# Two transformer blocks on one core: other places for three kinds of work, and two heads' last products in turn

## The chip, the core and the metric

The kernel runs on one core of a Trainium2 chip. The metric is device time in microseconds (us), the median of several executions. Five engines work side by side, each through its own list of instructions in a fixed order: TensorE (PE, matmuls; its weight loads are shown apart as PEld), VectorE (DVE), ScalarE (ACT), GpSimd (POOL) and SyncE (SP, which only issues transfers). [...]

## The reference

Two blocks of two layers each follow each other on 512 tokens of 1024 features. A layer of the first block mixes tokens in three branches (a gated matrix memory, a linear recurrence, sparse attention), merges them and applies a feed-forward network; a layer of the second block attends (over itself and over 256 memory tokens) and applies another one.

```python
for l in range(2):                                   # first block
    h = rms_norm(x, norm_mix[l]);  p = h @ w_in[l]   # split into 14 parts
    y_a = mlstm(...);  y_b = gelu(r_g) * rg_lru(conv(r_x), ...)   # recurrence: a scan over tokens
    score = sum_h w[t,h] * relu(q_idx[t,h] . k_idx[s])            # top 128 keys of each token
    y_c[h] = softmax(mask(q[h] @ k[h].T / 8)) @ v[h]              # 8 heads of 64 features
    x = x + (g_a*(y_a@wb0) + g_b*(y_b@wb1) + g_c*(y_c@wb2)) @ w_out[l]
    h = rms_norm(x, norm_ffn[l]);  g, u = split(h @ ffn_up[l])    # 2 x 3072
    x = x + (gelu(conv(g)) * u) @ ffn_down[l]
x = rms_norm(x, norm_final);  mem_n = rms_norm(mem, mem_norm)     # 256 x 1024
for i in range(2):                                   # second block
    x = x + concat(mixer(x), memory_attention(x, mem_n @ w_mem_kv[i])) @ w_out[i]
    g, u = split(rms_norm(x, norm_ffn[i]) @ w_gate_up[i])         # 2 x 2816
    x = x + (silu(g) * u) @ w_down[i]
```

## The kernel before

Features lie on the 128 partitions and tokens along the free axis, so x is eight tiles of 128x512. Each large product is made in three passes: operand and weight are split into a high part (`wh`, made on ACT, line 361) and a rest (`wl`, DVE, line 369), and `three` (line 436) issues rest by high, high by rest and high by high (line 433). Small exact products go through `mm32` (line 421), transposes through `turn` (line 425). Weights come in pieces of 128x1024 into 8 buffers `raw`; a piece is split into one of 3 pairs `wh`, `wl` some units ahead of its use.

The order on every engine is made while the program is built. Each piece of work is a generator (a chain) with a priority (a low number goes first). `Issue` holds the operations that are ready, with a cost from a formula for each helper (`scan` has 0.00104 us an element, `mm32` four passes at 2400 columns a us), and always issues the one that can start first by these costs, among near equals the one of the best priority. So a cost or a priority changes the order everywhere behind it. `main` (in `drive`) issues the units of weights one after the other, in the order in which `body` yields them; `loader` and `splitter` run up to 8 units ahead.

The feed-forward network (`ffn`, line 1969) multiplies a block of 256 columns of gate and up with 7 products instead of 8 (units P1 to P7, 24 matmuls each). P1, P5, P6 and P4 of a block use one buffer: after the split for P1, `dma_add` (line 416, on the queue of POOL) adds another piece of weights to it in place, P5 can be split when that has landed, and so on. When two blocks are done, their four tiles `ff` are the operand of the second projection (`down_units`, ps_t): its pieces of 24 matmuls (two output tiles, four operand tiles) are put between later P units, at the places that the list `first` gives.

`dsa_pair` (line 1554) handles two of the eight sparse heads: scores ps_at (the two heads in turn, on partitions 0 to 63 and 64 to 127 of the operands), probabilities `pr`, transposes ps_pt into `pT`, products ps_y with `av`; head 0 writes partitions 0 to 63 of the bank ps_y, head 1 the others. `rg_chain` (line 1317) is the recurrence; its products are ps_rg. `mem_prep` (line 2113) prepares the memory: four loads, a norm, 16 transposes ps_mem. ps_st and ps_bc are the sums of squares and the spreading of a norm.

## Time and profile before

| | |
|---|---|
| median of 3 runs | 3227.7 us (3225.82 to 3227.99) |
| the profiled execution | 3223.32 us, its span 3221.5 us |
| PE busy | 3167.3 us, 98% of the span |
| DVE, ACT, POOL busy | 2305.4, 1587.9, 403.3 us (72%, 49%, 13%) |
| share of the chain that ended last | PE 86%, DVE 9%, issue 2%, ACT 1% |
| moved by DMA | 397.39 MB, mean 123 GB/s |

PE is the engine to look at: 54.2 us of the span are left in which it does not work. Times in the rows further down are us from the start of the span unless ns is said. A line of the timeline gives start, duration, engine, line, output and inputs, shape and count, and in brackets how long the engine was idle before and what ended that.

### The profile page before, as it was taken

Reading aid. Unit: us, or ns where it says so; the run is one execution under the profiler, and the core shown is the slowest. Engines: PE = TensorE matmul, PEld = TensorE weight load, DVE = VectorE, ACT = ScalarE, POOL = GpSimd, SP = SyncE. Lnnn points to the kernel's source line nnn. Section 1 sums busy time; section 2 is a strip of 40 time slices with the busy share of each in tenths; the row PEclk is TensorE's granted clock in tenths of the full one; section 3 lists DMA queues with packets and bytes.
Section 4 is the critical chain, followed back from the end, with each engine's and each line's share of the span. In section 5 each row is a group of like instructions: output and inputs, shape, how many; then the busy total and the mean of one; then the engine's idle time right before and its main releaser. Section 6 shows DMA issues by size and latency. Waiting matters only on the chain.

```text
span 3221.5 us, 47254 instructions
## 1 busy us (share of the span) xinstructions
PE 3167.3 (98%) x18213; PEld 2712.2 (84%) x18213; DVE 2305.4 (72%) x4454; ACT 1587.9 (49%) x2650; POOL 403.3 (13%) x439
## 2 busy tenths in 40 slices
PE   8999999999999999999999999999999999999999
PEld 6778778989987778778989988888999988889998
DVE  7974444777787974445778787787777767777775
ACT  6552433544445552334544456877443457664443
POOL 2000000211100010000211112120211211011110
PEclk9999999999999999999999999999999999999999
DMA  5323233777752323233878753232887742257883
GB/s 155 98 73 92 68 90 101 156 169 159 175 142 76 105 72 92 67 98 98 167 162 175 167 133 118 62 99 57 173 176 165 185 151 72 66 115 173 176 175 82
DMA packets 367249, 397.39 MB, mean 123 GB/s; under 512 B 18031, under 2 KB 341344, under 8 KB 367024
## 3 DMA queue, kind: packets, MB, share of 16 engines
q1 hardware_dynamic: 262256, 276.47, 28.1%
q0 software_dynamic: 104736, 117.90, 21.9%
q8 instruction: 143, 2.34, 0.3%
q14 instruction: 82, 0.67, 0.1%
q10 hardware_dynamic: 32, 0.01, 0.0%
HBM read 383.83 MB, written 10.49 MB: 122 GB/s over the span
## 4 chain that ended last, share of the span: by engine, by line
PE 86%; DVE 9%; issue 2%; ACT 1%; DMA 0%; SPq 0%; POOL 0%; DVEq 0%; POOLq 0%; ACTq 0%
PE ps_t L433 38%; PE ps_u L433 26%; PE ps_n L433 11%; PE ps_at L433 2%; DVE wl L369 2%; PE ps_y L433 2%; PE ps_pt L425 2%; PE ps_y L421 1%; DVE m L1243 1%; DVE score L1244 1%; DVE u L369 1%; ACT pr L361 1%; DVE pr L1551 1%; PE ps_num L421 1%; PE ps_S L421 1%
## 5 line engine op out<-in xcount | busy, mean ns | idle before, releaser
L361 ACT ACTIVATE wh<-raw 128x1024 fp32r<-128x1024 f32 (+2 forms) x671 | 698.0, 1041 | 1020.0 <-PE ps_t L433 496.5
L369 DVE TENSOR_TENSOR wl<-raw,wh 128x1024 fp32r<-128x1024 f32 (+2 forms) x671 | 804.9, 1200 | 474.1 <-ACT wh L361 470.1
L433 PE MATMUL ps_u<-xsh,wl 128*128 128x256 f32 x1472 | 415.9, 283 | 11.0 <-DVE wl L369 8.0
L433 PE MATMUL ps_u<-xsh,wh 128*128 128x256 f32 x1472 | 414.9, 282 | 0.0
L433 PE MATMUL ps_u<-xsl,wh 128*128 128x256 f32 x1472 | 414.8, 282 | 0.0
L433 PE MATMUL ps_t<-ffl,wh 128*128 128x512 f32 x736 | 293.2, 399 | 3.8 <-DVE ffl L369 3.7
L433 PE MATMUL ps_t<-ffh,wl 128*128 128x512 f32 x736 | 289.1, 397 | 6.3 <-ACT ffh L361 5.7
L433 PE MATMUL ps_t<-ffh,wh 128*128 128x512 f32 x736 | 291.6, 396 | 0.0
L433 PEld LDWEIGHTS ps_u<-xsh,wl 128*128 128x128 f32 x1472 | 278.6, 189 | 13.7 <-issue 7.8
L433 PE MATMUL ps_t<-h2h,wl 128*128 128x512 f32 x704 | 280.6, 399 | 0.0
L433 PE MATMUL ps_t<-h2h,wh 128*128 128x512 f32 x704 | 280.3, 398 | 0.0
L433 PE MATMUL ps_t<-h2l,wh 128*128 128x512 f32 x704 | 279.9, 398 | 0.0
L433 PEld LDWEIGHTS ps_u<-xsl,wh 128*128 128x128 f32 x1472 | 278.6, 189 | 0.0
L433 PEld LDWEIGHTS ps_u<-xsh,wh 128*128 128x128 f32 x1472 | 278.6, 189 | 0.0
L369 DVE TENSOR_TENSOR x<-x,ps_t 128x512 f32<-128x512 f32 x232 | 158.2, 685 | 154.5 <-PE ps_t L433 152.7
L416 POOL DMA_DIRECT2D raw<-in_ffn_up_dram x96 | 122.7, 1328 | 748.4 <-DVE wl L369 513.4
L433 PE MATMUL ps_u<-xbh,wl 128*128 128x256 f32 x736 | 206.9, 281 | 1.5 <-DVE wl L369 1.5
L433 PE MATMUL ps_u<-xbl,wh 128*128 128x256 f32 x736 | 206.9, 281 | 0.0
L433 PE MATMUL ps_u<-xbh,wh 128*128 128x256 f32 x736 | 206.5, 281 | 0.0
L416 POOL DMA_DIRECT2D raw<-in_w_gate_up_dram x88 | 112.4, 1321 | 624.4 <-DVE wl L369 408.8
L433 PEld LDWEIGHTS ps_t<-ffl,wh 128*128 128x128 f32 x736 | 138.9, 189 | 39.3 <-DVE ffl L369 10.5
L433 PEld LDWEIGHTS ps_t<-ffh,wl 128*128 128x128 f32 x736 | 138.2, 189 | 38.9 <-ACT ffh L361 10.5
(449 smaller groups left out, 7068.1 us busy)
## 6 DMA issues: line engine op xcount, KB each, us to landing
raw<-in_w_in_dram SPq DMA_DIRECT2D x128, 512.0 KB, 3.8
raw<-in_ffn_up_dram SPq DMA_DIRECT2D x96, 512.0 KB, 4.3
raw<-in_ffn_up_dram POOLq DMA_DIRECT2D x96, 512.0 KB, 6.1
raw<-in_w_gate_up_dram SPq DMA_DIRECT2D x88, 512.0 KB, 4.5
raw<-in_w_gate_up_dram POOLq DMA_DIRECT2D x88, 512.0 KB, 6.3
raw<-in_w_out_dram SPq DMA_DIRECT2D x40, 512.0 KB, 3.5
raw<-in_ffn_down_dram SPq DMA_DIRECT2D x36, 512.0 KB, 4.6
raw<-in_w_down_dram SPq DMA_DIRECT2D x32, 512.0 KB, 4.8
```

Source lines behind the costliest of these rows:

```text
L361: lambda: nc.scalar.activation(out=out, in_=in_, func=func, **kw),
L369: dve(0.00104, lambda: nc.vector.tensor_tensor(out=out, in0=in0, in1=in1, op=op), [out], [in0, in1])
L416: order.op("pool", 1.0, lambda: nc.gpsimd.dma_start(out=out, in_=in_, accum_op=ALU.add), [out], [out], extra=max(n, 0.05), slack=-1.0)
L421: lambda: nc.tensor.matmul(o, lhsT=lhsT, rhs=rhs, start=start, stop=stop), [o], [lhsT, rhs],
L425: order.op("pe", 0.107, lambda: nc.tensor.transpose(o, in_, idn), [o], [in_, idn], rows=in_.shape[0])
L433: lambda: nc.tensor.matmul(o, lhsT=lhsT, rhs=rhs, start=first, stop=last, **kw), [o], [lhsT, rhs],
L1243: dve(0.00104, lambda: nc.vector.max(out=m8, in_=acc), [m8], [acc])
L1244: dve(0.00104, lambda: nc.vector.match_replace(out=acc, in_to_replace=m8, in_values=acc, imm_value=MARK), [acc], [acc, m8])
L1551: dve(0.00104, lambda: nc.vector.tensor_tensor_reduce(out=o, in0=v, in1=m, scale=1.0, scalar=NEG, op0=ALU.add, op1=ALU.max, accum_out=top) ...
```

## The change

Six edits. `scan` costs 0.0022 an element in the order's formula. `rg_chain` starts when the four tiles of the gate `rgt` are there too, and no longer waits for them in its middle. In `dsa_pair` both heads' probabilities are transposed first, then the products are issued key tile by key tile with the heads in turn, and their cost in the formula is halved. The first group of pieces of the second projection begins one place later. P1 of block 2 stands two units earlier. The chain that prepares the memory has priority 6, not 2.

```diff
     def scan(out, d0, d1, op0, op1):
-        dve(0.00104, lambda: nc.vector.tensor_tensor_scan(...
+        dve(0.0022, lambda: nc.vector.tensor_tensor_scan(...
-    def mm32(o, lhsT, rhs, start=True, stop=True):
-        order.op("pe", 4 * max(64, size(rhs)) / 2400.0,
+    def mm32(o, lhsT, rhs, start=True, stop=True, beside=1):
+        order.op("pe", 4 * max(64, size(rhs)) / 2400.0 / beside,
         def rg_chain():
-            yield from until(lambda: "bds" in st)
+            yield from until(lambda: "bds" in st and len(rgt) == 4)
...
-            while len(rgt) < 4:
-                yield "wait"
...
-            for j, rg in enumerate(rgs):
-                pT = {}
+            pT = {}
+            for j in range(2):
                 for grp in (((0, 0),), ((1, 0),), ((2, 0), (3, 256))):
...
-                if j == 0:
-                    while len(banks.left) <= 2:
-                        yield "wait"
-                    py = banks.take(F32, "ps_y")
-                for sb in range(NT):
-                    N = T - sb * P
-                    v = b.t[:, (0 if sb == 2 else 256):][:, 0:N] if sb >= 2 else pT[sb].t[:, 0:N]
+            py = yield from gbank("ps_y", 2)
+            for sb in range(NT):
+                o = 256 if sb == 3 else 0
+                for j, rg in enumerate(rgs):
                     h = 2 * hp + j
-                    mm32(py.t[rg, sb * P:T], av[sb].t[:, h * 64:(h + 1) * 64], v, sb == 0, sb == NT - 1)
-                for p_ in (pT[0], pT[1], b):
-                    p_.free()
-                yield
+                    mm32(py.t[rg, sb * P:T], av[sb].t[:, h * 64:(h + 1) * 64], pT[j, min(sb, 2)].t[:, o:o + T - sb * P],
+                         sb == 0, sb == NT - 1, beside=2)
+            for p_ in pT.values():
+                p_.free()
+            yield
...
         first = [places.index((e + 2, "P7")) if e + 2 < nblk else len(places) - 1 for e in done[:-1]]
+        first[0] += 1
...
-                      (0, "P3"), (1, "P6"), (0, "P4"), (2, "P1"), (1, "P3"), (2, "P2"), (2, "P5"), (1, "P4"), (3, "P1"),
+                      (0, "P3"), (2, "P1"), (1, "P6"), (0, "P4"), (1, "P3"), (2, "P2"), (2, "P5"), (1, "P4"), (3, "P1"),
...
-        spawn(g(), 2)
+        spawn(g(), 6)
```

No instruction is added or taken away on PE, DVE and POOL; on ACT two loads of function tables fewer are left (32 for 34). What moves is shown at three places.

On PE, the first pair of sparse heads, with the numbers of the buffers kept (ps_y is one bank, `pT` six different buffers in the changed kernel). Before:

```order
L421 MATMUL ps_y_3358<-pT_3340,av_1166 64x512
L421 MATMUL ps_y_3358<-pT_3341,av_1167 64x384
L421 MATMUL ps_y_3358<-pT_3348,av_1168 64x256
L421 MATMUL ps_y_3358<-pT_3348,av_1169 64x128
L425 MATMUL ps_pt_3365<-ident_71,pr_3223 128x128
```

The changed kernel, at the same place:

```order
L422 MATMUL ps_y_3383<-pT_3339,av_1166 64x512
L422 MATMUL ps_y_3383<-pT_3367,av_1166 64x512
L422 MATMUL ps_y_3383<-pT_3340,av_1167 64x384
L422 MATMUL ps_y_3383<-pT_3368,av_1167 64x384
L422 MATMUL ps_y_3383<-pT_3347,av_1168 64x256
L422 MATMUL ps_y_3383<-pT_3380,av_1168 64x256
L422 MATMUL ps_y_3383<-pT_3347,av_1169 64x128
L422 MATMUL ps_y_3383<-pT_3380,av_1169 64x128
```

The four products of head 0, which stood alone with head 1's transposes behind them, now alternate with those of head 1.

On SP, the loads of weights from the last mixing product of layer 0 to the start of its feed-forward network (up is the P units, down the second projection). Before:

```order
L410 DMA raw<-in_w_out_dram 128x4x256 x8
L410 DMA raw<-in_ffn_up_dram 128x4x256 x12
L410 DMA raw<-in_ffn_down_dram 128x4x256
L410 DMA raw<-in_ffn_up_dram 128x4x256
L410 DMA raw<-in_ffn_down_dram 128x4x256
L410 DMA raw<-in_ffn_up_dram 128x4x256 x3
L410 DMA raw<-in_ffn_down_dram 128x4x256
```

In the changed kernel:

```order
L410 DMA raw<-in_w_out_dram 128x4x256 x8
L410 DMA raw<-in_ffn_up_dram 128x4x256 x13
L410 DMA raw<-in_ffn_down_dram 128x4x256
L410 DMA raw<-in_ffn_up_dram 128x4x256 x3
L410 DMA raw<-in_ffn_down_dram 128x4x256
L410 DMA raw<-in_ffn_up_dram 128x4x256
L410 DMA raw<-in_ffn_down_dram 128x4x256 x2
```

The first piece of the second projection moves behind two more P units (P2 and P5 of block 3), and two pieces stand together at the third place; the other three feed-forward networks move alike.

On PE, the end of the first block, where the memory is prepared for the first time. Before:

```order
L425 MATMUL ps_mem<-ident,mem 128x128 x4
L433 MATMUL ps_t<-ffl,wh 128x512
L433 MATMUL ps_t<-ffh,wh 128x512
L425 MATMUL ps_mem<-ident,mem 128x128 x4
L421 MATMUL ps_st<-ones,nacc 128x1 x4
L433 MATMUL ps_n<-wh,hl 128x384
L433 MATMUL ps_n<-wl,hh 128x384
```

In the changed kernel, the first ps_st (behind the last ps_t stand 30 rows ps_n, of which the last three are shown):

```order
L434 MATMUL ps_n<-wh,hl 128x384
L434 MATMUL ps_n<-wl,hh 128x384
L434 MATMUL ps_n<-wh,hh 128x384
L422 MATMUL ps_st<-ones,nacc 128x1 x4
L434 MATMUL ps_n<-wh,hl 128x384
```

The norm's sums come behind 30 products of the next projection, and the transposes ps_mem behind both ps_st.

## Rows read from the trace of the kernel before

**Rows 1.** The page: span, and busy time of the engines.
```profile
span 3221.5 us, 47254 instructions
...
PE 3167.3 (98%) x18213; PEld 2712.2 (84%) x18213; DVE 2305.4 (72%) x4454; ACT 1587.9 (49%) x2650; POOL 403.3 (13%) x439
```

**Rows 2.** Whom PE waited for: us in total, times, longest.
```profile
PE ps_u L433 <- DVE wl L369: 9.5, 10, 2.5
PE ps_t L433 <- ACT ffh L361: 5.7, 2, 2.9
PE ps_rg L421 <- DVE rx L373: 4.1, 3, 2.0
...
PE ps_st L421 <- DVE nacc L369: 3.3, 1, 3.3
...
PE ps_b L425 <- DVE grow L369: 2.6, 2, 1.5
```

**Rows 3.** PE's timeline at the first pair of sparse heads.
```profile
377.59 0.40 PE L433 MATMUL ps_t<-h2h,wh 128*128 128x512 f32 x1
377.92 2.37 PE L421 MATMUL ps_y<-pT,av 128*64 128x512 f32 x8
380.22 1.31 PE L425 MATMUL ps_pt<-ident,pr 128*128 128x128 f32 x10
...
384.23 2.70 PE L421 MATMUL ps_at<-rT 64*128 64x128 f32 x40
386.86 0.51 PE L433 MATMUL ps_t<-h2h,wh 128*128 128x512 f32 x1
```

**Rows 4.** Instructions on the bank ps_y: ns shortest/median/longest, starts, forms.
```profile
L421 PEld LDWEIGHTS ps_y<-pT,av x128: 132/137/137, 377.9 to 1442.1; 128*64 128x64 f32 x128
L421 PE MATMUL ps_y<-pT,av x128: 272/432/644, 377.9 to 1442.2; 128*64 128x512 f32 x32, 128*64 128x384 f32 x32, 128*64 128x256 f32 x32, 128*64 128x128 f32 x32
```

**Rows 5.** The chain that ended last, in time: start, us, what.
```profile
229.91 4.46 PE ps_num L421 x40
...
684.25 5.57 PE ps_t L433 x24
689.82 5.65 PE ps_u L433 x48
```

**Rows 6.** PE's timeline, waits early in the feed-forward networks.
```profile
641.77 0.36 PE L433 MATMUL ps_u<-xsh,wl 128*128 128x256 f32 x1 [1.12 <-DVE wl L369]
...
645.28 0.39 PE L433 MATMUL ps_u<-xsh,wl 128*128 128x256 f32 x1 [0.45 <-DVE wl L369]
...
654.04 0.73 PE L433 MATMUL ps_t<-ffh,wl 128*128 128x512 f32 x2 [2.88 <-ACT ffh L361]
...
2306.81 0.55 PE L433 MATMUL ps_u<-xsh,wl 128*128 128x256 f32 x1 [2.52 <-DVE wl L369]
...
2919.88 0.36 PE L433 MATMUL ps_u<-xsh,wl 128*128 128x256 f32 x1 [2.34 <-DVE wl L369]
```

**Rows 7.** Busy by stretch: PE, PEld, DVE, ACT, POOL, then granted clock, DMA share.
```profile
637.00:655.00 18.00, 13.49 (x95) 11.81 (x94) 17.05 (x26) 9.55 (x13) 3.86 (x4) 0.99 0.88 191
...
654.65:658.06 3.41, 3.35 (x9) 2.37 (x9) 1.42 (x3) 0.63 (x1) 0.00 (x0) 0.50 1.22 193
...
1938.06:1944.88 6.82, 6.82 (x28) 6.32 (x26) 3.34 (x12) 0.76 (x3) 2.02 (x2) 0.50 0.29 77
...
2306.70:2310.11 3.41, 3.30 (x15) 3.33 (x16) 3.41 (x5) 1.74 (x2) 1.26 (x1) 0.50 0.31 39
```

**Rows 8.** Timelines of ACT, POOL and DVE before the wait that ends at 2306.81.
```profile
2292.16 1.06 ACT L361 ACTIVATE wh<-raw 128x1024 fp32r<-128x1024 f32 x1 [1.40 <-DMA raw<-in_w_gate_up_dram]
...
2294.78 1.26 POOL L416 DMA_DIRECT2D raw<-in_w_gate_up_dram  x1 [7.88 <-DVE wl L369]
...
2305.45 1.22 DVE L369 TENSOR_TENSOR wl<-raw,wh 128x1024 fp32r<-128x1024 f32 x1
```

**Rows 9.** Line 386, scans on DVE: ns shortest/median/longest, starts, forms.
```profile
L386 DVE TENSOR_TENSOR_SCAN grow<-zero,lsr x2: 1212/1212/1212, 69.4 to 1034.1; 4x512 f32<-4x512 f32 x2
```

## The prediction

> **What bounds the kernel now.** I read the page first: PE is busy 3167.3 of 3221.5 us [rows 1], so whatever is to be won is either PE work that gets shorter or part of the 54.2 us in which PE waits. The reader is to see in that row that no other engine comes near: an edit that only spares DVE or ACT is worth nothing by itself. Second I read whom PE waited for [rows 2]. Five of those lines make 25.2 us, and each belongs to a place that an edit touches: weights that are not split yet (ps_u on `wl`), tiles of the feed-forward network that are not ready for the second projection (ps_t on `ffh`), the recurrence's input (ps_rg), a norm's sum (ps_st), the rows of a scan (ps_b). [...]

> The sum is made against the profiled execution's own 3223.3 us; the median of the runs shown, 3227.7, lies 4.4 above it, and the forecast is put on the median.

> **A: two heads in turn.** This is the only edit that can shorten PE's work. A head's four products are eight rows that hold PE from 377.92 to 380.22, 2.30 us [rows 3]; 128 rows [rows 4] are 16 such blocks, 36.8 us. They use 64 of 128 columns of the array. What the trace does not have is two such halves in turn. Its nearest rows are the scores ps_at, whose two heads alternate on the two halves of the rows: 40 rows of 128 columns take 2.63 us, from 384.23 to 386.86 [rows 3], while 40 rows of the same length that use the whole array take 4.46 [rows 5], so halves in turn take 0.59 of the time. If halves of the columns do as halves of the rows, two heads take 4.60 x 0.59 = 2.71 us and each of eight pairs saves 1.89: 15.1 us. A block also costs 0.1 us at its start (0.33 from 377.59 to 377.92, where a matmul of 512 columns takes 5.57 / 24 = 0.23 [rows 3, 5]), and eight blocks fewer save 0.8. Together 15.9; I take 16, because ps_at is the nearest row. Best case, two heads in the time of one: 18.4 + 0.8 = 19.2. No overlap: 0.8. The loss on the other side is the third rival. Head 0's products now come after head 1's transposes; projections ps_t stand between, so nothing new ends last there.

> [...]

> **B: pieces of the second projection one place later, in the two networks of the first block.** Between 637 and 655 us DVE is busy 17.05 of 18 us while PE works 13.49 [rows 7]: PE waits 1.12, 0.45 and 2.88 us there [rows 6], because the tiles for the first piece come through DVE. Two more P units now stand in front of that piece. They give PE 5.65 us of work [rows 5] and ask DVE for two splits of 1.22 [rows 8], so DVE's arrears shrink by 5.65 - 2.44 = 3.2 of 4.45 us; the longest wait falls to about 1 us, behind which I expect no fall of the clock, another 1.7. Of these 4.9 I take 4.0, since the two units have outputs that pass through DVE as well. Both networks: 8. Bounds: nothing, if the arrears only move to P2 and P5 of block 3, and 6.1 each, all waits and the clock.

> **C: P1 of block 2 two units earlier, in all four networks.** In the second block's networks PE waits 2.52 and 2.34 us for P6 of block 2 [rows 6]. The chain behind it is one buffer that P1, P5 and P6 use in turn with a transfer that adds weights between. P5's split waited 1.40 us for such a landing at 2292.16; the next addition was issued at 2294.78 and the split that PE waited for ended at 2306.67 [rows 8]. P1 two units or 5.65 us earlier takes the 1.40 away, and the rest of the chain moves up by that: 1.4 us, and with a wait of about 1 left, the 1.7 of the clock. 3.1 each, 6 in all. What is late next is the addition behind P5. Bounds: nothing and 4.2 each.

> **D: the memory's preparation after the norm.** At the end of the first block PE waits 3.3 us for the sums of the norm [rows 2], and the clock's loss is 3.4 [rows 7]. Now 30 matmuls of the next projection stand ahead of the sums; from 384 columns, at three quarters of the 0.23 above, that is 5 us of work, more than the wait. But the norm's factor comes later too, and four banks of products wait for it before the next four can start. I take 4.5 of 6.7; bounds nothing and 6.7.

> **E: the recurrence later.** The three waits of 4.1 us go [rows 2]: PE has some 22 us of projections before the products now. All eight stand in one row, and their banks have to be emptied by ACT meanwhile; I leave 0.6 for that. 3.5; bounds nothing and 4.1.

> **F: the scan's cost.** A scan of 512 takes 1.21 us [rows 9] where the formula had 0.60, so the transposes behind it stood too early, 2.6 us of waiting in two places [rows 2]. They move behind one score product in layer 0 and two in layer 1. I take 1; bounds nothing and 2.6.

> **G: the re-sorted rest.** The changed order runs through the whole list, the second block's attention above all, where nothing was aimed at. 29 us of waits lie outside the five lines (54.2 - 25.2). I charge a fifth, 6 us, for waits of the same kind that come back elsewhere; bounds -5 and +15. The instructions themselves, and what DMA moves, stay the same.

> Sum: -16 - 8 - 6 - 4.5 - 3.5 - 1 + 6 = -33. That makes 3190 for the profiled execution and 3195 on the median.

> **Rivals.** First, the halves of the columns do not run together, and A is 0.8. For it: every row in rows 4 has all 128 rows of the array, and the two operands have to stream in at once, which no row shows; against it: ps_at. The rest stands: 3195 + 15 = 3210.

> Second, the waits in the networks only move. For it: in 637 to 655 DVE is all but full and the share of DMA is 0.88 [rows 7]; the piece that goes later is the one that asks least of both. Against it: the 3.2 us worked out above. B and C are then nothing: 3195 + 14 = 3209. With the first rival at once it is 3224, no change.

> Third, slower: taking halves in turn makes PE empty itself at each change of half. A matmul of 128 columns lasts 272 ns by rows 4, where one of 40 holds PE 112 ns [rows 5]; 160 ns are its way through the array, otherwise hidden, and a weight load of 137 is hidden as well. If each of the 128 rows pays both, A is +38.0 and the whole 3195 + 16 + 38 = 3249. It decides from 0.13 us a row on, since all the rest of the sum is 17 us. Against it: 40 rows of ps_at that change half each time without it.

> [...]

> **How the numbers follow.** My forecast, with more or less of B to G, has 0.62 and reaches from 3181 to 3206 by itself. The first rival has 0.13, the second 0.15, both together 0.05, the third 0.05. The range 3177 to 3213 leaves out the third, both together and the ends of the first case, under 2 in 10. Faster means more than 0.2%, about 6.5 us, which is what can be told apart from no change: 0.62 + 0.13 + 0.15, less a little where G is at its upper end, 0.89. Within 0.2%: 0.06. Slower: 0.05.

> **What would show it.** A: a pair's products on ps_y take 2.7 us from their start to the next row, 16 rows; 4.6 says first rival, over 5 the third. B: no wait over 1.2 us on `ffh`, and no 0.50 in the clock near 650. C: waits under 1.3 us before P6 of block 2. D: no wait of ps_st on the sums, and full clock behind it. E: ps_rg waits for nothing on DVE. F: ps_b waits 1 us or less in layer 0. G: PE's idle time is 54 less 16 to 20 us. The forecast is wrong if PE's busy time does not fall by 12 us or more, or if waits that I don't name make over 12 us.

## The result, and the profile after

| | median us | ratio to the kernel before, 95% interval |
|---|---|---|
| before | 3226.8 (3223.6 to 3228.0) | |
| changed | 3186.7 (3181.6 to 3189.4) | 0.9876 (0.9858 to 0.9893) |

The change saves 40 us, 1.24%; the forecast was 3195. The profiled execution took 3185.49 us, 37.8 less than that of before. First the page of the changed kernel, busy time by engine and shares of the chain that ended last, then whom PE waited for (us in total, times, longest); they answer to [rows 1, 2]. The last fence is the line of the kernel before that [rows 2] does not show.

```profile
PE 3142.0 (99%) x18213; PEld 2700.4 (85%) x18213; DVE 2300.4 (72%) x4454; ACT 1585.0 (50%) x2648; POOL 404.1 (13%) x439
```

```profile
PE 91%; DVE 6%; ACT 1%; issue 1%; DMA 0%; SPq 0%; POOL 0%; ACTq 0%; DVEq 0%; POOLq 0%
```

```profile
PE ps_u L434 <- DVE u L369: 7.6, 12, 0.9
PE ps_t L434 <- ACT ffh L361: 4.7, 3, 2.2
...
PE ps_b L426 <- DVE grow L369: 2.1, 2, 1.2
...
PE ps_u L434 <- DVE wl L369: 1.6, 4, 0.5
```

```profile
PE ps_u L433 <- DVE u L369: 3.0, 8, 0.5
```

PE has 91% of the chain, DVE 6, for 86 and 9 before. PE's work fell by 25.3 us (3167.3 to 3142.0) and its idle time by 12.6 (54.2 to 41.6). The lines on ps_rg and ps_st of [rows 2] are gone, the one on `wl` fell from 9.5 to 1.6; `ps_u <- DVE u`, where PE waits for a bank that DVE has not read yet, rose from 3.0 to 7.6 and now stands on top. The other half of the reading is where the span got shorter, from the start of the first score ps_at and of the first and last P unit (ps_u) of each network in both traces:

| stretch | change, us | predicted |
|---|---|---|
| start to first ps_at, layer 0; last ps_u to first ps_at, layer 1 | -4.2; +0.8 | E, F: -4.5 |
| first ps_at to first ps_u, layers 0 and 1 | -9.7; -9.7 | A: -16 |
| networks of the first block | -1.9; -1.2 | B: -8 |
| last ps_u of layer 1 to the second block's first network | -6.1 | D: -4.5 |
| networks of the second block | -2.2; -3.5 | C: -6 |
| the rest | -0.1 | G: +6 |

A's place, PE's timeline at the first pair of sparse heads (start, us, line, operation, count), answers to [rows 3]:

```profile
375.92 2.37 PE L422 MATMUL ps_y<-pT,av 128*64 128x512 f32 x16
378.23 2.65 PE L422 MATMUL ps_at<-rT 64*128 64x128 f32 x40
```

Sixteen rows take 2.31 us from their start to the next, where eight took 2.30. And the places of B and C, waits in brackets, which answer to [rows 6]:

```profile
644.29 0.72 PE L434 MATMUL ps_t<-ffh,wl 128*128 128x512 f32 x2 [2.22 <-ACT ffh L361]
```
```profile
2247.04 0.39 PE L434 MATMUL ps_u<-xsh,wl 128*128 128x256 f32 x1 [0.87 <-DVE u L369]
```
```profile
2259.48 0.39 PE L434 MATMUL ps_u<-xsh,wl 128*128 128x256 f32 x1 [0.85 <-DVE u L369]
```

The wait for the first piece of the second projection is 2.22 for 2.88 us, less relief than forecast. Before P6 of block 2 the 2.52 us are gone, and 1.72 us of waits for banks have come in the same network. The windows (columns as in [rows 7]) show the stretch behind the first of these waits, and that the one before it is as full of DVE work as ever:

```profile
627.00:645.20 18.20, 15.92 (x119) 14.63 (x119) 17.14 (x26) 9.47 (x12) 2.57 (x2) 1.00 1.00 216
...
645.60:649.01 3.41, 3.41 (x9) 2.45 (x9) 1.27 (x3) 0.63 (x1) 0.00 (x0) 0.50 0.21 66
```

The granted clock is still 0.50 behind it: PE's rows of 512 columns start 0.43 us apart there (645.66, 646.09, 646.51), where 24 of them took 5.57 us, 0.23 each, in [rows 5].

**A number for the clock.** Executions of one kernel differ in their mean granted clock: the changed kernel's four took 3181.6 us at 0.997, 3185.5 at 0.996, 3187.9 and 3189.4 at 0.995. With the share that the clock did not grant (to three digits) taken off, the four spans are 3170 to 3172 us. So below, beside the median, each profile's span is also given less half the length of its stretches at 0.50 (1.7 us for one of 3.41): 3221.5 - 15.4 = 3206.1 before, 3183.6 - 12.9 = 3170.7 after. This is an estimate; where PE waits during such a stretch it takes off too much, and I hold it good to some 2 us.

### The profile page after: what moved, and what is told of

Same layout as the page of the kernel before. It is cut to its first block, busy times and chain, and to the rows that moved or that the text cites. A ratio compares the mean times of both kernels' runs of the same rounds, so it can differ in the third digit from the quotient of the medians.

```text
span 3183.6 us, 47249 instructions
## 1 busy us (share of the span) xinstructions
PE 3142.0 (99%) x18213; PEld 2700.4 (85%) x18213; DVE 2300.4 (72%) x4454; ACT 1585.0 (50%) x2648; POOL 404.1 (13%) x439
## 3 DMA queue, kind: packets, MB, share of 16 engines
q8 instruction: 143, 2.34, 0.3%
## 4 chain that ended last, share of the span: by engine, by line
PE 91%; DVE 6%; ACT 1%; issue 1%; DMA 0%; SPq 0%; POOL 0%; ACTq 0%; DVEq 0%; POOLq 0%
PE ps_t L434 40%; PE ps_u L434 26%; PE ps_n L434 14%; PE ps_at L434 2%; PE ps_y L434 2%; PE ps_pt L426 2%; DVE wl L369 2%; DVE u L369 1%; DVE pr L1550 1%; PE ps_y L422 1%; ACT pr L361 1%; PE ps_num L422 1%; PE ps_sc L422 1%; PE ps_S L422 1%; PE ps_qt L426 0%
```

## The experiments

**1. The sparse pairs alone**, on the kernel before: `mm32` and `dsa_pair` as changed, nothing else.

```diff
-        order.op("pe", 4 * max(64, size(rhs)) / 2400.0,
+        order.op("pe", 4 * max(64, size(rhs)) / 2400.0 / beside,
...
-            for j, rg in enumerate(rgs):
-                pT = {}
+            pT = {}
+            for j in range(2):
```

> The kernel before with the edit of the sparse pairs alone (both heads' transposes first, the 16 products in turn, their cost in the order's formula halved). Theory: column halves of the array run together entirely, so 8 pairs save 18.4 us and up to 0.8 at their starts; time 19 us under the kernel before, about 3208; between the first ps_at and the feed-forward network each first-block layer is 9.7 us shorter, and nothing else moves by more than 1.5 us. Rival (the other edits' new order makes part of the gain of 9.7 per layer): under 13 us in all, 3214 or more.

Measured: 3201.7 us, ratio 0.9926 (0.9913 to 0.9940). The two stretches from the first ps_at to the network are 9.8 and 9.7 us shorter, as in the changed kernel; the span is 21.9 shorter, and 20.3 without the falls. A is a term by itself, and its size is that of the best case. That nothing else moves by more than 1.5 us was not met at two places: the start of layer 0 is 2.0 us longer, and the last network 2.0 shorter, 1.7 of it a fall of the clock that is not there. The median fell further than expected, partly because the profiled execution of before, 3223.3, is at the lower end of its own (3222.3 to 3228.2).

**2. The same 16 products head by head**, on the changed kernel.

```diff
-            for sb in range(NT):
-                o = 256 if sb == 3 else 0
-                for j, rg in enumerate(rgs):
+            for j, rg in enumerate(rgs):
+                for sb in range(NT):
+                    o = 256 if sb == 3 else 0
```

> The changed kernel with the same 16 products of a pair issued head by head (8 of head 0, then 8 of head 1... each head's four tiles one after the other) with everything else, the halved cost in the formula too, as in the changed kernel. Theory (overlap by turns): each pair's products on ps_y take 4.6 us where they take 2.3, the time is 18 us above the changed kernel, about 3205. Rival (the gain is from grouping the transposes and leaving one bank for both heads, not from turns): within 4 us of the changed kernel, about 3187.

Measured: 3197.6 us, 0.9910 (0.9897 to 0.9924), 11 us above the changed kernel (12.3 by spans without the falls). It lies between the two numbers, and the timeline tells why:

```profile
377.69 3.93 PE L422 MATMUL ps_y<-pT,av 128*64 128x512 f32 x16
381.54 2.64 PE L422 MATMUL ps_at<-rT 64*128 64x128 f32 x40
```

A pair takes 3.85 us, neither 4.6 nor 2.3. The single records in this group (every tile is two rows) show head 1 starting early:

```
head 0, rows 1 to 8: 377.685 378.165 378.594 378.917 379.239 379.455 379.671 379.780
head 1, rows 1 to 8: 379.245 379.725 380.154 380.477 380.799 381.015 381.231 381.340
```

Head 1's first row starts 6 ns after head 0's fifth, ahead of three older rows. The halves thus overlap even without turns, over the last 0.74 us; the turns give the other 1.54 x 8 = 12.3 us. A row four places further on can start with the older one, but no sooner: that was the guess for runs 3 and 4, and run 4 shows where it is too strict.

**3 and 4. Turns of two and of three key tiles**, on the changed kernel: the two loops over tiles and heads (the lines that run 2 takes away) replaced by a list of (head, tile).

```diff
+            for j, sb in ((0, 0), (0, 1), (1, 0), (1, 1), (0, 2), (0, 3), (1, 2), (1, 3)):
...
+            for j, sb in ((0, 0), (0, 1), (0, 2), (1, 0), (1, 1), (1, 2), (0, 3), (1, 3)):
```

> The changed kernel with the heads' turns two key tiles long: the products of head 0 for tiles 0 and 1 (4 rows), of head 1 for the same, then both for tiles 2 and 3. Theory (from the run with the products head by head, where head 1's first row started 6 ns after head 0's fifth, three rows before head 0's last: a row can pass up to three older rows that wait for the other half of the columns): the first four rows of head 1 start with head 0's second row at the latest, a pair takes 2.3 to 2.8 us instead of 2.31 and the time is within 4 us of the changed kernel. Rival (only the last 0.64 us of a turn, whatever its rows, can be shared): a turn of 4 rows shares 0.64 of 1.5 us, a pair takes 3.0 us or more, 5 us or more above the changed kernel.

> The changed kernel with turns of three key tiles (6 rows of head 0, 6 of head 1, then 2 and 2). Theory (a row starts no earlier than the row four before it in the list): head 1's first row starts with head 0's third, 0.91 us after its first, and all of head 1 follows it: a pair takes 0.91 + 2.30 = 3.2 us for 2.31, and 8 pairs make the kernel 7 us slower than the changed one, about 3194. Rival (a fixed time is shared at each change of half, 0.74 us as in the run head by head, whatever the rows): head 1's first row starts some 1.3 us after head 0's first, a pair takes 3.6 us or more, 3197 or more.

Measured: 3187.5 us, 0.9881 (0.9867 to 0.9896), and 3194.7, 0.9905 (0.9891 to 0.9918). The pair in each:

```profile
377.15 2.42 PE L422 MATMUL ps_y<-pT,av 128*64 128x512 f32 x16
379.51 0.71 PE L422 MATMUL ps_at<-rT 64*128 64x128 f32 x8
```
```profile
377.20 3.28 PE L422 MATMUL ps_y<-pT,av 128*64 128x512 f32 x16
380.41 2.64 PE L422 MATMUL ps_at<-rT 64*128 64x128 f32 x40
```

Turns of four rows take 2.36 us, as good as turns of two. With turns of six head 1 starts at 378.115, 6 ns after head 0's third row at 378.109, and a pair takes 3.21 us for the 3.2 expected. Both rivals are out: a pair takes 2.31, 2.36, 3.21 and 3.85 us with turns of two, four, six and eight rows. But "no earlier than the row four before it" is not quite what run 4 shows. In each of its eight pairs head 0's last row, the fourteenth of the list, starts some 52 ns before the tenth (in the first pair at 379.295 and 379.347). In the records of all three runs rows start ahead of three older rows, and none ahead of more.

**5. The networks alone**, on the kernel before.

```diff
+        first[0] += 1
...
-                      (0, "P3"), (1, "P6"), (0, "P4"), (2, "P1"), (1, "P3"),
+                      (0, "P3"), (2, "P1"), (1, "P6"), (0, "P4"), (1, "P3"),
```

> The kernel before with only the two edits of the feed-forward networks (P1 of block 2 two units earlier, the second projection's first group one place later). Theory from the trace after (the arrears of DVE near 650 move but do not shrink): first-block networks 1 to 2 us shorter each, second-block networks 2 to 3.5 each, 9 us in all, about 3218; the clock still falls to 0.50 near 650 and 1610. Rival (the steps of the prediction, hidden in the changed kernel by another effect of the sparse edit): 14 us, about 3213, no fall of the clock there. Second rival: the waits only move, 3224 or more.

Measured: 3218.9 us, 0.9977 (0.9968 to 0.9986). The size in all is that of the first theory; by network it is 2.7, 2.4, 1.8 and 3.5 us, where 1 to 2 were expected of each of the first two. Behind the ffh waits its profile shows no fall of the clock, though the waits are the same 2.2 us as after: that part of the expectation missed. Behind waits of this length the profile after shows 0.50 and this one does not.

**6. The pieces one place later alone**, on the kernel before.

```diff
+        first[0] += 1
```

> The kernel before with only the pieces of the second projection one place later. Theory of the prediction's step on it (arrears of DVE shrink by the 3.2 us worked out, the waits for ffh of 2.88 go and with them the 0.50 clock behind them near 655 and 1614): 4.0 us per first-block network, 8 in all, about 3218.5. Rival (the arrears only move to P2 and P5 of block 3, or the edit needs the other place of P1): 3224 or more, a wait of over 1.2 us remains between 640 and 665.

Measured: 3217.1 us, 0.9978 (0.9968 to 0.9988). The networks of the first block are 3.8 and 3.5 us shorter. PE's waits in the first of them, and DVE and the clock in the stretch where the 0.50 of before stood:

```profile
PE ps_t L433 <- DVE ffl L369: 3.0, 6, 0.5
PE ps_u L433 <- DVE wl L369: 2.0, 3, 1.1
PE ps_u L433 <- DVE u L369: 0.9, 2, 0.5
```
```profile
654.65:658.06 3.41, 3.04 (x14) 2.16 (x13) 3.34 (x5) 1.36 (x4) 0.00 (x0) 1.00 1.15 237
```

No line on `ffh` is left, and the clock stays at 1.00. B alone does what the prediction said, to the size; by the estimate above, 1.7 of each network's gain is the fall of the clock that is gone. Run 5, with P1 moved as well, is no faster than this one.

**7. The pieces at their old place**, on the changed kernel.

```diff
-        first[0] += 1
```

> The changed kernel with the second projection's first group at its place of before. Theory of the prediction (one place later is worth 4.0 us per first-block network): 8 us above the changed kernel, 3195. Theory from the trace after (the arrears only shrank from 4.5 to 3.1 us per network): 2 to 4 us above, 3189 to 3191. Rival: no difference within 2 us, the whole gain in those networks is from P1.

Measured: 3193.3 us, 0.9900 (0.9886 to 0.9915), 6.6 above the changed kernel. The wait for the first piece:

```profile
642.39 1.22 PE L434 MATMUL ps_t<-ffh,wl 128*128 128x512 f32 x2 [5.48 <-ACT ffh L361]
```

This is the run that settles B. With P1 moved and the pieces not, the wait is 5.48 us, 2.60 more than the 2.88 of before [rows 6]. From there the later pieces take 3.26 off, the 3.2 of the prediction's working. The networks of the first block are 3.2 us longer each than in the changed kernel, and the falls of the clock at their waits last 6.83 us where they lasted 3.41. The theory from the trace after, that the arrears hardly shrink, was wrong; P1 had raised them first.

**8. P1 one unit earlier instead of two**, on the changed kernel, in all four networks.

```diff
-                      (0, "P3"), (2, "P1"), (1, "P6"), (0, "P4"), (1, "P3"),
+                      (0, "P3"), (1, "P6"), (2, "P1"), (0, "P4"), (1, "P3"),
```

> The changed kernel with P1 of block 2 only one unit earlier than in the kernel before (between P6 of block 1 and P4 of block 0), in all four networks. Theory: P5's split needed 1.4 us and one unit is 2.8, so P6 of block 2 still waits for nothing over 0.5 us, while the new waits of 0.85 and 0.5 us for banks that DVE empties (7.6 us in 12 places) fall by half: 4 us under the changed kernel, about 3183. Rival: DVE is as much in arrears wherever P1 stands, the waits change their names: within 2 us of the changed kernel.

Measured: 3182.4 us, 0.9867 (0.9853 to 0.9882). PE's waits:

```profile
PE ps_t L434 <- ACT ffh L361: 5.3, 3, 2.5
PE ps_u L434 <- DVE u L369: 4.2, 8, 0.9
```

The bank waits fell from 7.6 to 4.2 us, as expected, but the first piece now waits 2.5 us. The four networks together are 4.2 us shorter than in the changed kernel, 2.5 without the one fall that is missing in them. The whole span without the falls is 2.0 us above the changed kernel's; the difference lies outside the networks and is at the limit of what this number can tell. So the number was met, but only some 2.5 us of it by the reason expected; the rest goes with the clock (0.996 to 0.999 in its four executions).

**9. The pieces two places later**, on the changed kernel.

```diff
-        first[0] += 1
+        first[0] += 2
```

> The changed kernel with the second projection's first group two places later instead of one. Theory: the waits of 2.2 us on ffh in both first-block networks go, DVE has another 2 units' time; 4 us less, or 6 with the clock behind them, 3181 to 3183. Rival (DVE is full there, its arrears then hold up P2, P5 and P4): within 2 us of the changed kernel.

Measured: 3188.1 us, 0.9886 (0.9869 to 0.9902): the rival. PE waits 8.8 us for `wl` in place of 1.6:

```profile
PE ps_u L434 <- DVE wl L369: 8.8, 6, 3.6
```

Past one place the arrears do move into the next units.

**10 and 11. P1 moved in the second block alone**, by two units (run 10, below) and by one (run 11: `head.insert(11 if ...`), on the changed kernel. Networks of the second block have 11 blocks of columns (`nblk`), those of the first 12.

```diff
+        head = [(0, "P1"), (1, "P1"), (0, "P2"), (1, "P2"), (0, "P5"), (0, "P7"), (1, "P5"), (0, "P6"), (1, "P7"),
+                (0, "P3"), (1, "P6"), (0, "P4"), (1, "P3"), (2, "P2"), (2, "P5"), (1, "P4"), (3, "P1"), (2, "P6")]
+        head.insert(10 if nblk == 11 else 12, (2, "P1"))
```

> The changed kernel with P1 of block 2 at its place of before in the two first-block networks, two units earlier still in the two second-block networks; the pieces one place later everywhere. Theory (P1 two units earlier puts 2.6 us of arrears on DVE in front of the first piece in the first-block networks, and the later pieces take 3.3 back): the ffh waits of 2.2 us there and the bank waits of 0.49 and 0.85 go, 2 to 3.5 us less per network, 4 to 7 in all, 3180 to 3183; P6 of block 2 waits again for its weights by 0.5 us or less. Rival (pieces one place later only push the arrears into P2 and P5 of block 3, as two places later did): within 2 us of the changed kernel.

> The kernel of the run before this one, with P1 of block 2 one unit earlier instead of two in the second-block networks. Theory: another 0.5 to 1.3 us per second-block network without the clock, since half of the bank waits of 0.85 go there: 1 to 3 us under that run, about 3179. Rival: the same as that run within 1.5 us, since one wait only takes the name of another.

Measured: 3182.5 us, 0.9864 (0.9848 to 0.9881), and 3178.9, 0.9854 (0.9839 to 0.9868). The first piece in run 11, with the wait in brackets:

```profile
645.10 0.50 PE L434 MATMUL ps_t<-ffl,wh 128*128 128x512 f32 x1 [0.37 <-DVE ffl L369]
```

The waits for `ffh` are gone in both runs, and with them the falls near 645 and 1594. In the first block P6 of block 2 waits for its weights again, 1.1 us in both, where 0.5 or less was expected of run 10. Run 10 keeps the bank waits of C in the second block, run 11 loses half of them. Run 11 is the best of all: its four executions, 3178.2 to 3179.5, lie below the fastest of the changed kernel, 3181.6. The two were not timed side by side and their intervals overlap, so that it beats the changed kernel is likely, not settled.

**12. Memory, recurrence and scan alone**, on the kernel before.

```diff
-        dve(0.00104, lambda: nc.vector.tensor_tensor_scan(...
+        dve(0.0022, lambda: nc.vector.tensor_tensor_scan(...
-            yield from until(lambda: "bds" in st)
+            yield from until(lambda: "bds" in st and len(rgt) == 4)
...
-        spawn(g(), 2)
+        spawn(g(), 6)
```

> The kernel before with only the memory's priority, the later start of the recurrence and the scan's cost. Theory: 4 us less before the first ps_at of layer 0, 6 us less between the networks of layer 1 and the first network of the second block, 10 us in all, about 3217; the 0.50 clock at 1938 is gone. Rival: the gain of the memory stage came from the shorter attention in front of it (loads had more time), then 5 us or less in all, 3222 or more.

Measured: 3211.1 us, 0.9953 (0.9941 to 0.9966); its profiled execution was the longest of its five, a span of 3211.8, 9.7 us less than before. Without the falls the starts of both layers are 2.9 and 2.4 us shorter and the stretch before the second block's networks 3.9; with them that stretch is 5.6 shorter, and the 0.50 of [rows 7] at 1938 has no counterpart. The rival (5 us or less) is out.

The spans of runs 1, 5 and 12 fell by 21.9, 4.2 and 9.7, together 35.8, the changed kernel's by 37.9: by these profiles the three groups of edits add up. By the medians they are 24.8, 7.6 and 15.4, together 47.7 for the 40.1 of the changed kernel; in ratios the gap is 0.20%, inside the 0.27% that the four intervals leave together. So that they add up is shown to some 8 us only. Inside the networks B and C do not add up, as the next section tells.

## Why the prediction was right, and where not

The sum came out 4.9 us short of the span's 37.9, and that it is so near is in part luck: G's charge of 6, which did not come, stands against the 4.9 that B gave less in the changed kernel, and A gave 3.4 more.

**A** was the right mechanism with a term too small: 16 forecast, 19.4 measured, just over its best case of 19.2. The step that failed is "if halves of the columns do as halves of the rows": I carried the 0.59 of ps_at over, and the columns gave 2.31 / 4.60 = 0.50. What ps_at loses beside that is open; its rows have 128 columns, these up to 512. (The 4.46 us that it was compared with come from the chain; from their first start to the next row those 40 rows take 4.38 us, which would make it 0.60.) The first and third rival fell by the 2.31 us: 16 rows, each with its own weight load of 132 to 137 ns, 2.2 us of loads in all, took no longer than the 2.30 of 8 rows with 8 loads [rows 3, 4].

**B** was right as a mechanism: 4.0 per network, 3.8 and 3.5 by itself, 3.3 of waiting from C's starting point. In the changed kernel both its signs failed all the same (a wait of 2.22 us on `ffh`, 0.50 in the clock at 645.60), and the networks gave 1.9 and 1.2: that is C's doing. The second rival fell by runs 6 and 7, but it is what happens one place further on (run 9). No run shows by itself what a fall of the clock costs: the 1.7 in B and C and the 3.4 in D are half of the 3.41 and 6.82 us at 0.50 [rows 7], an estimate; rows of 512 columns, 0.43 us apart at 0.50 for 0.23, make it 1.6 for 3.41 us.

**C** is where a step failed. "3.1 each, 6 in all" for the second block measured 2.2 and 3.5; 1.7 of each is the fall of the clock that is gone, so the waits gave 0.5 and 1.8 for the 1.4, since new waits for banks took some of it back. But the edit acts in all four networks, and for the first block's I set it at nothing, without a reason. There it costs 4.2 us: B and C together gave 1.9 and 1.2, where B alone gives 3.8 and 3.5. Of these 4.2, 3.4 are the two falls of the clock behind the waits of 2.2 us (0.50 from 645.6 and from 1594.5, 3.41 us each): without the falls the changed kernel loses 0.2 and 0.6 to run 6, and run 5, which has the same waits and no fall there, 1.1 in each. The windows 30 to 40 us after the network's start (columns as in [rows 7], the third pair is DVE), in the changed kernel and then in run 6:

```profile
603.10:613.10 10.00, 9.48 (x81) 9.28 (x79) 6.48 (x10) 4.14 (x5) 2.57 (x2) 1.00 1.17 205
```
```profile
616.80:626.80 10.00, 10.00 (x87) 10.00 (x86) 7.75 (x13) 3.68 (x5) 2.57 (x2) 1.00 0.96 177
```

DVE is busy 6.48 us for 7.75: P1 stands in front of P4 of block 0, whose outputs feed the convolution, so DVE has less to do here and does it later; in run 5 it is 6.48 too. Block 0's last `ffl` ends 59.0 us after the network's start for 55.5, and in 613 to 645 DVE is all but full (30.1 of 32 us). Runs 7 and 8 agree: one unit or two, the wait stays while P1 is ahead of P4. Run 10, which puts it back, takes the wait away. The prediction had asked only what the moved unit needs, not what now stands behind it, though it had read DVE as full 20 us later [rows 7].

**D** gave 6.1 for 4.5, close to its bound of 6.7; the wait of ps_st is gone, and the clock is 1.00 from 1890 to 1950. The stretch holds an attention layer as well, in which two falls (2042 and 2110) stand for one before (2143); without the falls it is 4.4 (in run 12 5.6, without the falls 3.9). **E and F**: no wait of ps_rg, ps_b still 1.16 us in layer 0 (forecast 1 or less). Together 3.4 for 4.5, but two new falls of the clock (1024 and 1164) stand in layer 1; without the falls it is 5.2. **G** was charged 6 and is 0: outside the five lines of [rows 2] PE waits 33.2 us for 29.0, but 4.6 of that are the waits for banks in the networks, which belong to C; the others did not grow. PE's idle time fell by 12.6, not by the 16 to 20 forecast, because of C in the first block and the new bank waits.

## What to carry to other kernels

Where two products each use 64 of the array's 128 columns, try issuing them alternately: here the second head added 0.01 us to the 2.30 of the first with turns of two rows, 0.06 with turns of four, 0.91 with six and 1.55 with eight. When a unit of work is moved forward on the engine that bounds the kernel, list what it pushes back and who must digest that next: the move is free only if the engine behind has room later, not if it has room now (here DVE was busy 6.48 of 10 us where P1 went in, and 30.1 of the 32 us behind). And when two edits meet in one place, work out the second from the state that the first leaves: each alone and both together need three runs.
